# Reordering the seven products of a Strassen-type group, and the transfers around them, in a two-layer decoder trunk

## The chip, the cores and the metric

The kernel runs on one core of a Trainium2 chip. The metric is the device time of one execution in microseconds (us), the median of several runs. The core's engines work in parallel, each through its own queue in order: PE (TensorE, matrix products, with its weight loads shown as PEld), DVE (VectorE), ACT (ScalarE), POOL (GpSimd) and SP (SyncE, here only a queue that issues transfers). Transfers (DMA) are issued from SP and POOL and run on sixteen DMA engines.

## The reference, cut to what matters

Two layers of a decoder trunk on one sequence of 256 tokens with 1024 features, all in f32. Each layer is a half-weighted gated feed-forward (ffn1), a token mixer, a cross attention to a memory, and a second feed-forward (ffn2); each is preceded by an RMS norm and added to x:

```python
def swiglu(x, w_gate, w_up, w_down):
    return (jax.nn.silu(x @ w_gate) * (x @ w_up)) @ w_down

for l in range(DEPTH):                                   # DEPTH = 2
    x = x + 0.5 * swiglu(rmsnorm(x, ffn1_norm[l]), ffn1_w_gate[l], ffn1_w_up[l], ffn1_w_down[l])
    h = rmsnorm(x, mix_norm[l])
    x = x + (even_mixer(h, ...) if l % 2 == 0 else odd_mixer(h, ...))
    x = x + memory_cross_attention(rmsnorm(x, xa_norm[l]), mem_n, xa_w_q[l], xa_w_kv[l], xa_w_o[l])
    x = x + 0.5 * swiglu(rmsnorm(x, ffn2_norm[l]), ffn2_w_gate[l], ffn2_w_up[l], ffn2_w_down[l])
return rmsnorm(x, final_norm)
```

The hidden width of a feed-forward is 2816 = 22 x 128. The change lies in two of the four feed-forwards: ffn2 of layer 0 and ffn1 of layer 1, which follow one another.

## The kernel before, in words

**Weights.** All weights of the run are cut into 128x128 tiles and stored in HBM in the order of their use, in chunks of 16 tiles (1 MB). The class `Stream` loads chunk after chunk through SP's queue into four buffers `raw` and splits them block by block (8 tiles, 128x1024) into a high part `whi` (ACT, line 142) and the rest `wlo` (DVE, line 143). There are five buffers of each, so the splits run at most four blocks ahead of PE. A product of f32 values is made of three matmuls, high by high, low by high and high by low.

**A feed-forward stage** (`ffn`). Hidden features are made in groups of four tiles (f0 = 0, 4, 8, 12, 16) and a last group of two (f0 = 20). Of a group, the function `hidden` makes gate and up with the tokens on the partitions; each is cut into four parts of two row blocks (lines 560 to 562, 12 matmuls a part, cost 2600 ns with the planner). ACT applies the silu to the gate (line 581), DVE multiplies it with up. The result must then be turned, so that features lie on the partitions: `turned_back` transposes 32x32 blocks on DVE (line 531), writes the tile to HBM from POOL's queue (`turn`, line 533), reads it back with blocks exchanged in four transfers (line 535), and, some time later, splits it into the tiles h that the second product needs (ACT line 543, DVE line 544). The turned tile lies in one of two buffers, `v` or `kT`, in turns. This split is pinned in the order of ACT's and DVE's queues: what is behind it waits for it. The time at which it is put there is the delay given to `pe.after`. Then the down part multiplies h with the down weights (lines 417 and 418, the last column 422 to 424): four columns of x over the first 16 h tiles, the same four over h[16..19], over h[20..21], and then the other four whole.

**The seven products.** In the two stages named, group f0 = 12 is made with seven products instead of eight (Winograd's form): tokens are halved, input features are halved, and the two outputs (gate, up) stand as the other pair, so the weights are four quarters w11 (gate, upper rows), w21 (gate, lower rows), w12 (up, upper rows) and w22 (up, lower rows), a chunk of 1 MB each. Three products use a plain quarter, four use a sum of quarters. The sums are made by transfers of POOL's queue that add to what lies in the tile (line 617, `accum_op`): tile `one` (named k2) goes from w11 to w11+w12 to w11+w12+w22, tile `two` (named bias) from w12 to w12+w22, then w11 and w21 are added. These "added" chunks do not come through the stream. The inputs of four products are sums and differences of quarters of x (function `side`, lines 637 to 644), in buffers h. Each product is 12 matmuls into one bank `tr` (lines 665 to 667), and its result is kept in a tile h and combined on DVE and ACT (functions q1 to q7).

**What sets the order.** The class `Order` keeps a planned clock: fillers (the parts and products, in a written list) are emitted one after another, each advancing the clock by its cost, and tasks given to `after(delay, fn, cost)` are emitted before the first filler that starts at or after their due time. The list `ups` holds the parts of the groups 0, 4, 8, 16, 20; the seven products are inserted behind 10, 12, 14, 16, 18, 20 and 22 of the 36 parts. The framework's scheduler then may move instructions of one engine past each other, after a timing model of its own, unless an instruction is pinned with `tc.keep_in_program_order`: it then stays behind the instruction that was emitted before it on its engine.

Other users of the buffers: `bias` holds the values of the cross attention ahead of the first of the two stages, and behind the second the attention bias of the odd mixer (`load_bias`, line 1073, 1 MB read from `dists`); `k2` holds the keys of the cross attention.

Of the kernel before, what the change touches and what calls it, by code (L numbers as in the profile page):

```python
# [15 lines left out]
F32 = mybir.dt.float32  # L16
F32R = mybir.dt.float32r
AF = mybir.ActivationFunctionType
ALU = mybir.AluOpType
# [4 lines left out]
P = 128  # L24
D = 1024
KT = D // P
S = 256
FF = 2816
FT = FF // P
# [9 lines left out]
CHUNK = 16  # L39
# [225 lines left out]
def build(nc, tc, ctx, a):  # L265
# [18 lines left out]
    def w2():  # L284
        return act.tile([P, 512], F32, name="w2", bufs=6)
# [5 lines left out]
    x = consts.tile([P, KT, S], F32, name="x")  # L291
# [24 lines left out]
    def col(key, k):  # L316
        c = VCOL[key] + k
        return vecs[:, c:c + 1]
# [200 lines left out]
        nc.gpsimd.dma_start(out, tok.rearrange("(u q) f -> q u f", u=2))  # L519


    def ffn(which, layer, n, nxt, first=False, last=False):
        h = [None] * FT
        gate, up = f"{which}_w_gate", f"{which}_w_up"

        def turned_back(f0, s, c):

            t = act.tile([P, 8 * c * 32], F32, name=("v", "kT" if (which, layer) in AT else "k2")[f0 // 4 % 2], bufs=1)
            to = t.rearrange("p (b u c i) -> p u c b i", b=4, u=2, c=c)
            for u in range(2):  # L530
                nc.vector.transpose(to[:, u], s[u].rearrange("p (c b j) -> p c b j", c=c, b=4))
            d = dram.tile([P, 8 * c * 32], F32, name="turn", bufs=2)
            nc.gpsimd.dma_start(d, t)
            for b in range(4):
                nc.gpsimd.dma_start(t[32 * b:32 * b + 32].rearrange("j (a x) -> j a x", a=4),
                                   d.rearrange("(a j) (b x) -> b j a x", a=4, b=4)[b])
            back = t.rearrange("p (a u c i) -> p c u a i", a=4, u=2, c=c)

            def split():
                for i in range(c):  # L540
                    h[f0 + i] = x2 = h_tile()
                    hi, lo = (m.rearrange("p u (a i) -> p u a i", a=4) for m in (x2.hi, x2.lo))
                    tc.keep_in_program_order(nc.scalar.activation(hi, back[:, i], AF.Copy))
                    tc.keep_in_program_order(nc.vector.tensor_tensor(lo, back[:, i], hi.bitcast(F32), op=ALU.subtract))  # L544

            pe.after((18000 if (which, layer) in AT else 28000) if f0 < FT // 4 * 4 - 4 else 22000, split, 0)

        def rows_of(name, c, bank, evac, other=None):

# [49 lines left out]
                    rows_of(up, f0 * P, acc_tile, product))  # L599

        def seven(f0, at):

            at += 4
            w11, w21, w22 = (a["w"][ws.ring(at + 2 * i + 1)] for i in (2, 3, 5))
            w12 = a["w"][RING + list(AT).index((which, layer))]
            for p in range(4):
                for k in range(4):
                    ws.place.append((RING + list(AT).index((which, layer)), 4 * p + k,
                                     (up, layer, p * P, f0 * P + 2 * (k % 2 * P) + k // 2, 2)))
            one = act.tile([P, CHUNK * P], F32, name="k2", bufs=1)  # L610
            two = act.tile([P, CHUNK * P], F32, name="bias", bufs=1)
            nc.gpsimd.dma_start(one, w11)
            nc.gpsimd.dma_start(two, w12)
            done = []

            def add(t, w):
                tc.keep_in_program_order(nc.gpsimd.dma_start(t, w, accum_op=ALU.add))
# [12 lines left out]
            sides = {}  # L630

            def side(p):
                t, y = w2(), w1()[:, :P]
                s3, s1, s2, s4 = (t[:, i * P:(i + 1) * P] for i in range(4))
                g, gq = col(n.key, p), col(n.key, p + 4)
                (k0, k1), (q0, q1) = ((x[:, k, :P], x[:, k, P:]) for k in (p, p + 4))
                nc.vector.tensor_scalar(y, k1, g, None, op0=ALU.mult)
                nc.vector.scalar_tensor_tensor(s3, k0, g, y, op0=ALU.mult, op1=ALU.subtract)
                nc.vector.scalar_tensor_tensor(s1, q1, gq, y, op0=ALU.mult, op1=ALU.subtract)
                nc.vector.scalar_tensor_tensor(s2, q1, gq, s3, op0=ALU.mult, op1=ALU.add)  # L640
                nc.vector.scalar_tensor_tensor(s4, q0, gq, s2, op0=ALU.mult, op1=ALU.subtract)
                hi, lo = (act.tile([P, 512], F32R, name="h", bufs=FT) for _ in range(2))
                nc.scalar.activation(hi, t, AF.Copy)
                nc.vector.tensor_tensor(lo, t, hi.bitcast(F32), op=ALU.subtract)
                sides[p] = [[m[:, i * P:(i + 1) * P] for m in (hi, lo)] for i in range(4)]
# [12 lines left out]

            def product(left, evac, name=None, row=0):
                def go():  # L660
                    ps = tr_tile()
                    for p in range(4):
                        wh, wl = (paired(w) for w in ws.take(name, layer, row + p * P, f0 * P, 4))
                        xh, xl = left(p)
                        nc.tensor.matmul(ps, xh, wh, start=p == 0, stop=False)
                        nc.tensor.matmul(ps, xh, wl, start=False, stop=False)
                        nc.tensor.matmul(ps, xl, wh, start=False, stop=p == 3)
                    evac(ps)
                    ws.flush()

                return always, go, 2600

            def part(q, u):
                return lambda p: [n.x[p + 4 * q].v[:, u, m] for m in range(2)]

            def mixed(i):
                return lambda p: sides[p][i]
# [7 lines left out]
            def q7(ps):  # L685
                nc.scalar.activation(keep("q7"), ps, AF.Copy)
                add(two, w11)
                pe.after(10000, lambda: add(two, w21), 0)

            def q1(ps):  # L690
                nc.scalar.activation(keep("q1"), ps, AF.Copy)

            def q2(ps):
                s0 = keep("s0")
# [3 lines left out]
            def q6(ps):  # L698
# [6 lines left out]
            def q3(ps):  # L705
                t = kept["q1"]
                tt(t, ps, t, op=ALU.subtract)
                stt(t, t, r(0), kept["s0"], op0=ALU.mult, op1=ALU.mult)

            def q4(ps):  # L710
                t, u3 = kept["q5"], kept["q7"]
# [355 lines left out]
    def load_bias(which):  # L1067


        t = act.tile([P, 8, 256], F32, name="bias", bufs=1)  # L1070
        src = bass.AP(tensor=dists.tensor, offset=dists.offset + which * P * 8 * 384 + 127,
                      ap=[[8 * 384 - 1, P], [384, 8], [1, 256]])
        tc.keep_in_program_order(nc.gpsimd.dma_start(t, src))
        return t
# [341 lines left out]
```

## Time and profile before

| | |
|---|---|
| median of 3 runs | 980.32 us (979.98 to 980.7) |
| profiled execution | 980.3 us |
| its span, first to last instruction | 978.4 us, mean granted PE clock 0.993 |
| busy | PE 956.1 us (98%), PEld 872.4, DVE 715.3 (73%), ACT 573.3 (59%), POOL 130.0 (13%) |
| moved by DMA | 232.29 MB, 237 GB/s over the span |
| transfers issued from SP | 185.58 MB |
| transfers issued from POOL | 45.13 MB |

The profile's names leave out digits at the end: k2 is shown as k, w2 as w. A row of the timeline reads: start, duration, engine, line, operation, tile written <- tiles read, shapes, how often; in brackets the time that the engine was idle before it, and what ended that. A row of the waits reads: who waited on whom, us in all, times, longest. A row of stretches gives start and end, length, then busy us and instructions of PE, PEld, DVE, ACT and POOL, then the granted PE clock as a fraction, the share of the DMA engines in use, and GB/s. Lists of transfers give tile, queue, how many, size, and us from issue to landing.

### The profile page before, as it was taken

What the parts mean: (1) busy time and instruction counts of PE and PEld (TensorE: products, weight loads), DVE (VectorE), ACT (ScalarE), POOL (GpSimd) and SP (SyncE); (2) the same over time, 40 slices, a digit from 0 to 9 for tenths busy, and PEclk for the clock granted to TensorE, in tenths of its full rate; (3) what the DMA queues carried; (4) which work ended last, traced back from release to release, by engine and by line L of the source; (5) the groups of instructions that cost most, each with busy time, mean ns of one, the idle gap of its engine ahead of it and who ended that gap; (6) DMA issues with size and microseconds to landing.
All of it is one profiled execution on the core that took longest, in us unless ns stands there. A gap on an engine that the chain in (4) does not pass through costs nothing.

```text
span 978.4 us, 15160 instructions
## 1 busy us (share of the span) xinstructions
PE 956.1 (98%) x5808; PEld 872.4 (89%) x5808; DVE 715.3 (73%) x1152; ACT 573.3 (59%) x928; POOL 130.0 (13%) x229
## 2 busy tenths in 40 slices
PE   9999999999999899999999989999999999999997
PEld 8888899999999778879988867989999998888896
DVE  7667757888869769756967874766887797576673
ACT  7556545696657566544656545455786585555541
POOL 0411210001000121111011101100000005511210
PEclk9999999999999989999999999999999999999999
DMA  9899975545526899878679967955645357997831
GB/s 371 320 359 317 310 240 202 209 150 181 207 92 254 248 276 348 302 207 290 219 219 265 364 199 207 344 199 184 250 138 174 108 172 283 306 283 246 277 131 43
DMA packets 39191, 232.29 MB, mean 237 GB/s; under 512 B 5960, under 2 KB 6984, under 8 KB 14928
## 3 DMA queue, kind: packets, MB, share of 16 engines
q1 hardware_dynamic: 26784, 185.58, 52.8%
q0 software_dynamic: 11760, 45.13, 17.0%
q8 instruction: 45, 0.74, 0.3%
q10 hardware_dynamic: 576, 0.64, 0.2%
q14 instruction: 26, 0.21, 0.1%
HBM read 217.66 MB, written 16.80 MB: 240 GB/s over the span
## 4 chain that ended last, share of the span: by engine, by line
PE 75%; DMA 15%; issue 5%; DVE 2%; POOL 2%; ACT 1%; POOLq 0%; ACTq 0%; DVEq 0%
PE acc L561 8%; PE acc L560 7%; PE acc L562 7%; PE acc L422 7%; PE acc L424 7%; PE acc L423 7%; PE acc L417 6%; DMA turn<-kT 5%; DMA bias<-in_w 3%; DMA kT<-turn 3%; PE sc L417 3%; PE acc L418 3%; PE sc L560 2%; PE sc L561 2%; PE sc L562 2%
## 5 line engine op out<-in xcount | busy, mean ns | idle before, releaser
L143 DVE TENSOR_TENSOR wlo<-raw,whi 128x1024 fp32r<-128x1024 f32 (+2 forms) x373 | 419.2, 1136 | 149.4 <-ACT whi L142 146.8
L142 ACT ACTIVATE whi<-raw 128x1024 fp32r<-128x1024 f32 (+2 forms) x373 | 361.2, 982 | 236.4 <-PE acc L562 84.6
L561 PE MATMUL acc<-wlo,x 128*128 128x512 f32 x544 | 207.7, 382 | 3.0 <-DVE wlo L143 3.0
L560 PE MATMUL acc<-whi,x 128*128 128x512 f32 x544 | 203.5, 382 | 5.3 <-ACT whi L142 5.3
L562 PE MATMUL acc<-whi,x 128*128 128x512 f32 x544 | 206.5, 381 | 0.0
L560 PEld LDWEIGHTS acc<-whi,x 128*128 128x128 f32 x544 | 103.2, 190 | 21.4 <-ACT whi L142 7.1
L561 PEld LDWEIGHTS acc<-wlo,x 128*128 128x128 f32 x544 | 103.3, 190 | 19.8 <-DVE wlo L143 5.4
L562 PEld LDWEIGHTS acc<-whi,x 128*128 128x128 f32 x544 | 103.3, 190 | 14.5
L417 PE MATMUL acc<-h,whi 128*128 128x512 f32 x330 | 108.7, 382 | 2.4 <-DVE h L544 2.4
L418 PE MATMUL acc<-h,wlo 128*128 128x256 f32 x330 | 90.0, 273 | 0.0
L424 PE MATMUL acc<-h,wlo 128*128 128x256 f32 x322 | 87.7, 275 | 0.0
L423 PE MATMUL acc<-h,whi 128*128 128x256 f32 x322 | 87.7, 275 | 0.0
L422 PE MATMUL acc<-h,whi 128*128 128x256 f32 x322 | 86.5, 277 | 0.0
L424 PE MATMUL acc<-x,wlo 128*128 128x256 f32 x304 | 84.1, 278 | 0.0
L423 PE MATMUL acc<-x,whi 128*128 128x256 f32 x304 | 83.8, 277 | 0.0
L422 PE MATMUL acc<-x,whi 128*128 128x256 f32 x304 | 83.3, 278 | 0.0
L417 PEld LDWEIGHTS acc<-h,whi 128*128 128x128 f32 x330 | 62.4, 189 | 11.4 <-DVE h L544 2.7
L418 PEld LDWEIGHTS acc<-h,wlo 128*128 128x128 f32 x330 | 63.3, 192 | 0.1
L423 PEld LDWEIGHTS acc<-h,whi 128*128 128x128 f32 x322 | 61.7, 192 | 0.1
L424 PEld LDWEIGHTS acc<-h,wlo 128*128 128x128 f32 x322 | 61.7, 192 | 0.1
L422 PEld LDWEIGHTS acc<-h,whi 128*128 128x128 f32 x322 | 60.6, 192 | 0.4 <-DVE x L485 0.2
L423 PEld LDWEIGHTS acc<-x,whi 128*128 128x128 f32 x304 | 58.2, 192 | 0.2
(273 smaller groups left out, 1674.1 us busy)
## 6 DMA issues: line engine op xcount, KB each, us to landing
raw<-in_w SPq DMA_DIRECT2D x169, 1024.0 KB, 5.9
bias<-in_w POOLq DMA_DIRECT2D x8, 1024.0 KB, 14.5
turn<-v POOLq DMA_DIRECT2D x12, 512.0 KB, 3.4
v<-turn POOLq DMA_DIRECT2D x48, 128.0 KB, 6.1
k<-in_w POOLq DMA_DIRECT2D x6, 1024.0 KB, 10.4
dists<-line POOLq DMA_DIRECT2D x2, 1536.0 KB, 14.1
raw<-in_memT SPq DMA_DIRECT2D x3, 1024.0 KB, 4.9
raw<-in_w SPq DMA_DIRECT2D x7, 388.0 KB, 6.1
```

The costliest lines, as they stand in the source:

```text
L142: for ins in (self.nc.scalar.activation(hi[:, at], src, AF.Copy), self.nc.vector.tensor_tensor(lo[:, at], src, hi[:, at].bitcast(F32), op= ...
L143: self.nc.vector.tensor_tensor(lo[:, at], src, hi[:, at].bitcast(F32), op=ALU.subtract)):
L417: nc.tensor.matmul(ps, w[0], x2.both, start=start, stop=False)
L418: nc.tensor.matmul(ps[:, :S], w[1], x2.high, start=False, stop=stop)
L422: nc.tensor.matmul(ps[:, :S], w[0], x2.high, start=start, stop=False)
L423: nc.tensor.matmul(ps[:, :S], w[0], x2.low, start=False, stop=False)
L424: nc.tensor.matmul(ps[:, :S], w[1], x2.high, start=False, stop=stop)
L560: nc.tensor.matmul(ps[u], xh, wh, start=k == 0, stop=False)
L561: nc.tensor.matmul(ps[u], xh, wl, start=False, stop=False)
L562: nc.tensor.matmul(ps[u], xl, wh, start=False, stop=k == KT - 1)
```

## The change

- The products stand in another order, q1, q7, q2, q5, q3, q6, q4 instead of q5, q7, q1, q2, q6, q3, q4, and behind 4, 8, 10, 12, 16, 22 and 26 of the 36 parts.
- The first of them uses tile `one` while it still holds plain w11, so w11 is no longer loaded by the stream as well. w11 and w12 lie in two chunks of their own at the end (`RING`).
- The loads of `one` and `two` and the first sum (w12+w22) are in `load_bases`. For the first stage it is called at the stage's start, for the second 114 us (planned) into the first stage, there with all three pinned.
- The other sums are issued at the ends of q1, q7 (two of them, the second 18 us later) and q5.
- The mixed inputs are made in two halves, `side` at 8 us + 3.9 us a row block and `side2` at 32 us + 3.9 us; the first operation of each is pinned. q3 only copies its result, and q6 does the work that q3 did.
- The splits of turned tiles in these two stages stand 34 us behind the product for f0 = 0 and 4, 28 for f0 = 8 and 22 for 12, 16 and 20 (before: 18 for f0 below 16, 22 for the rest). The turned tile of f0 = 12 lies in k2 instead of kT.
- The read of the odd mixer's bias is planned 114 us into the second stage instead of 100 us.

```diff
+PLACES = (4, 8, 10, 12, 16, 22, 26)
-ADDED = {at + 4 + 2 * i + 1 for at in AT.values() for i in (0, 1, 4, 6)}
-RING = CHUNKS - len(AT)
+ADDED = {at + PLACES[i] // 2 + i for at in AT.values() for i in (0, 1, 3, 5, 6)}
+RING = CHUNKS - 2 * len(AT)
...
+    def load_bases(which, layer, pin):
+        w11, w12, w21, w22 = quarters(which, layer)
+        bases[which, layer] = tiles = [act.tile([P, CHUNK * P], F32, name=name, bufs=1) for name in ("k2", "bias")]
+        for t, w in zip(tiles, (w11, w12)):
+            ins = nc.gpsimd.dma_start(t, w)
+            if pin:
+                tc.keep_in_program_order(ins)
+        tc.keep_in_program_order(nc.gpsimd.dma_start(tiles[1], w22, accum_op=ALU.add))
...
-            t = act.tile([P, 8 * c * 32], F32, name=("v", "kT" if (which, layer) in AT else "k2")[f0 // 4 % 2], bufs=1)
+            t = act.tile([P, 8 * c * 32], F32, name=("v", "kT" if sevens and f0 != SEVEN else "k2")[f0 // 4 % 2], bufs=1)
...
-            pe.after((18000 if (which, layer) in AT else 28000) if f0 < FT // 4 * 4 - 4 else 22000, split, 0)
+            pe.after((34000 if f0 < 8 else 28000 if f0 < SEVEN else 22000) if sevens else
+                     28000 if f0 < FT // 4 * 4 - 4 else 22000, split, 0)
...
-            pe.after(6000, lambda: (add(one, w12), add(two, w22)), 0)
-            for i, t, n_added in ((0, one, 1), (1, two, 1), (4, one, 2), (6, two, 3)):
-                ws.sums[at + 2 * i + 1] = summed(t, n_added)
+            for i, t, n_added in ((0, one, 0), (1, two, 0), (3, one, 1), (5, one, 2), (6, two, 2)):
+                ws.sums[at[i]] = summed(t, n_added)
...
             def side(p):
                 t, y = w2(), w1()[:, :P]
-                s3, s1, s2, s4 = (t[:, i * P:(i + 1) * P] for i in range(4))
+                s3, s1 = (t[:, i * P:(i + 1) * P] for i in range(2))
...
+            def side2(p):
+                t = w2()
+                s2, s4 = (t[:, i * P:(i + 1) * P] for i in range(2))
...
             for p in range(4):
-                pe.after(8000 + 2600 * p, lambda p=p: side(p), 0)
+                pe.after(8000+3900*p, lambda p=p: side(p), 0)
+                pe.after(32000+3900*p, lambda p=p: side2(p), 0)
...
+            def q1(ps):
+                nc.scalar.activation(keep("q1"), ps, AF.Copy)
+                add(one, w12)
+
+            def q7(ps):
+                nc.scalar.activation(keep("q7"), ps, AF.Copy)
+                add(two, w11)
+                pe.after(18000, lambda: add(two, w21), 0)
...
-            return [product(mixed(1), q5), product(mixed(0), q7), product(part(0, 0), q1, gate),
-                    product(part(1, 0), q2, gate, 4 * P), product(mixed(2), q6), product(mixed(3), q3, up, 4 * P),
+            return [product(part(0, 0), q1), product(mixed(0), q7), product(part(1, 0), q2, gate, 4 * P),
+                    product(mixed(1), q5), product(mixed(3), q3, up, 4 * P), product(mixed(2), q6),
                     product(part(1, 1), q4)]
...
         if at is not None:
+            if (which, layer) == ("ffn2", 0):
+                load_bases(which, layer, False)
+                pe.after(114000, lambda: load_bases("ffn1", 1, True), 0)
             assert ws.taken == FIRST + at * CHUNK, (ws.taken, at)
             for i, f in enumerate(seven(SEVEN, at)):
-                ups.insert(8 + 2 + 3 * i, f)
+                ups.insert(PLACES[i] + i, f)
...
-    pe.after(100000, lambda: early.update(bias=load_bias(1)), 0)
+    pe.after(114000, lambda: early.update(bias=load_bias(1)), 0)
     ffn("ffn1", 1, n, nxt)
```

More of the change, by code (lines that the diff above doesn't have):

```diff
@@ L519, in to_tokens, with placed, quarters @@
         nc.gpsimd.dma_start(out, tok.rearrange("(u q) f -> q u f", u=2))
+    def placed(at):
+        return [at + o // 2 + i for i, o in enumerate(PLACES)]
+    def quarters(which, layer):
+        at, here = placed(AT[which, layer]), RING + 2 * list(AT).index((which, layer))
+        return [a["w"][c] for c in (here, here + 1, ws.ring(at[2]), ws.ring(at[4]))]
+    bases = {}
+    def load_bases(which, layer, pin):
[6 more added lines that the diff above has]
+        tc.keep_in_program_order(nc.gpsimd.dma_start(tiles[1], w22, accum_op=ALU.add))
     def ffn(which, layer, n, nxt, first=False, last=False):
@@ L524, in ffn @@
         gate, up = f"{which}_w_gate", f"{which}_w_up"
+        sevens = (which, layer) in AT
         def turned_back(f0, s, c):
-            t = act.tile([P, 8 * c * 32], F32, name=("v", "kT" if (which, layer) in AT else "k2")[f0 // 4 % 2], bufs=1)
+            t = act.tile([P, 8 * c * 32], F32, name=("v", "kT" if sevens and f0 != SEVEN else "k2")[f0 // 4 % 2], bufs=1)
             to = t.rearrange("p (b u c i) -> p u c b i", b=4, u=2, c=c)
@@ L601, in seven @@
         def seven(f0, at):
[L603 to L613, printed above, removed]
+            w11, w12, w21, w22 = quarters(which, layer)
+            at = placed(at)
+            for i, name in enumerate((gate, up)):
+                for p in range(4):
+                    for k in range(4):
+                        ws.place.append((RING + 2 * list(AT).index((which, layer)) + i, 4 * p + k,
+                                         (name, layer, p * P, f0 * P + 2 * (k % 2 * P) + k // 2, 2)))
+            one, two = bases[which, layer]
             done = []
@@ L624, in summed, with part_of @@
                 return ready
-            pe.after(6000, lambda: (add(one, w12), add(two, w22)), 0)
-            for i, t, n_added in ((0, one, 1), (1, two, 1), (4, one, 2), (6, two, 3)):
-                ws.sums[at + 2 * i + 1] = summed(t, n_added)
+            for i, t, n_added in ((0, one, 0), (1, two, 0), (3, one, 1), (5, one, 2), (6, two, 2)):
+                ws.sums[at[i]] = summed(t, n_added)
             sides = {}
+            def part_of(p):
+                return [(x[:, k, :P], x[:, k, P:], col(n.key, k)) for k in (p, p + 4)]
@@ L632, in side, with parted @@
+            def parted(t, at):
+                hl = act.tile([P, 512], F32R, name="h", bufs=FT)
+                hi, lo = hl[:, :S], hl[:, S:]
+                nc.scalar.activation(hi, t, AF.Copy)
+                nc.vector.tensor_tensor(lo, t, hi.bitcast(F32), op=ALU.subtract)
+                for i in range(2):
+                    sides[at[0], at[1] + i] = [m[:, i * P:(i + 1) * P] for m in (hi, lo)]
             def side(p):
                 t, y = w2(), w1()[:, :P]
-                s3, s1, s2, s4 = (t[:, i * P:(i + 1) * P] for i in range(4))
@@ L635, in side @@
-                g, gq = col(n.key, p), col(n.key, p + 4)
-                (k0, k1), (q0, q1) = ((x[:, k, :P], x[:, k, P:]) for k in (p, p + 4))
-                nc.vector.tensor_scalar(y, k1, g, None, op0=ALU.mult)
+                s3, s1 = (t[:, i * P:(i + 1) * P] for i in range(2))
+                (k0, k1, g), (q0, q1, gq) = part_of(p)
+                tc.keep_in_program_order(nc.vector.tensor_scalar(y, k1, g, None, op0=ALU.mult))
                 nc.vector.scalar_tensor_tensor(s3, k0, g, y, op0=ALU.mult, op1=ALU.subtract)
@@ L639, in side @@
                 nc.vector.scalar_tensor_tensor(s1, q1, gq, y, op0=ALU.mult, op1=ALU.subtract)
[L640 removed]
+                parted(t[:, :S], (p, 0))
+            def side2(p):
+                t = w2()
+                s2, s4 = (t[:, i * P:(i + 1) * P] for i in range(2))
+                (k0, k1, g), (q0, q1, gq) = part_of(p)
+                tc.keep_in_program_order(nc.vector.tensor_scalar(s2, k1, g, None, op0=ALU.mult))
+                nc.vector.scalar_tensor_tensor(s2, k0, g, s2, op0=ALU.mult, op1=ALU.subtract)
+                nc.vector.scalar_tensor_tensor(s2, q1, gq, s2, op0=ALU.mult, op1=ALU.add)
@@ L641, in side @@
                 nc.vector.scalar_tensor_tensor(s4, q0, gq, s2, op0=ALU.mult, op1=ALU.subtract)
[L642 to L645, printed above, removed]
+                parted(t[:, :S], (p, 2))
             for p in range(4):
-                pe.after(8000 + 2600 * p, lambda p=p: side(p), 0)
+                pe.after(8000+3900*p, lambda p=p: side(p), 0)
@@ L676, in mixed @@
             def mixed(i):
-                return lambda p: sides[p][i]
+                return lambda p: sides[p, i]
             tt, stt = nc.vector.tensor_tensor, nc.vector.scalar_tensor_tensor
+            def q1(ps):
[5 more added lines that the diff above has]
+                pe.after(18000, lambda: add(two, w21), 0)
             def q5(ps):
@@ L683, in q5, with q3 @@
                 add(one, w22)
[L685 to L691, printed above, removed]
+            def q3(ps):
+                nc.scalar.activation(keep("q3"), ps, AF.Copy)
             def q2(ps):
```

6 lines of the change are left out of this document (2 added, 4 removed).

## The prediction

> **What bounds the kernel now.** First I asked which engine the time belongs to: PE is busy 98% of the span (first row), and after the change it runs the same matmuls. So only places where PE waits, or runs at a lower clock, can give time. I read who PE waited for over the whole run, then cut the two changed stages (second feed-forward of layer 0, first of layer 1) at the first matmul of each part.
>
> ```profile
> PE 956.1 (98%) x5808; PEld 872.4 (89%) x5808; DVE 715.3 (73%) x1152; ACT 573.3 (59%) x928; POOL 130.0 (13%) x229
> ...
> PE acc L560 <- ACT whi L142: 5.3, 4, 3.3
> PE acc L561 <- DVE wlo L143: 3.0, 4, 0.8
> PE tr L665 <- ACT whi L142: 2.6, 2, 2.3
> PE acc L417 <- DVE h L544: 2.4, 1, 2.4
> PE tr L667 <- DVE h L644: 1.1, 1, 1.1
> ...
> 310.40:434.14 123.74, 117.04 (x520) 99.31 (x519) 90.24 (x125) 69.70 (x93) 18.26 (x28) 0.97 0.85 266
> 434.14:491.95 57.81, 57.81 (x376) 53.72 (x375) 46.38 (x73) 31.15 (x45) 5.47 (x10) 1.00 0.76 257
> 491.95:612.44 120.49, 114.35 (x521) 98.64 (x519) 84.84 (x113) 66.76 (x87) 16.48 (x27) 0.99 0.82 253
> 612.44:672.96 60.52, 58.08 (x376) 53.73 (x374) 42.58 (x62) 30.34 (x43) 6.26 (x11) 1.00 0.70 252
> 528.40:549.10 20.70, 20.70 (x97) 18.12 (x97) 17.67 (x21) 13.49 (x18) 1.42 (x2) 1.00 1.01 313
> ```
>
> The window rows give length, then busy time of PE, weight load, DVE, ACT and POOL, then PE's clock, DMA share and GB/s. Rows one and two are the up part and down part of the first stage, three and four those of the second. The last is undisturbed: 8 slots (a slot is 12 matmuls: half a quarter of an ordinary group, or one of the seven products) in 20.70 us, 2.59 us a slot. An up part has 36+7 = 43 slots, so 43 x 2.59 = 111.3 us, and 0.1 for two transposes. The losses are 123.74-111.4 = 12.3 and 120.49-111.4 = 9.1; the second down part is 60.52-57.81 = 2.7 us longer than the first, which has no PE wait. Together 24.1 us: the ceiling of what this change can give.
>
> Next I looked at what ACT, which works in order, stood in front of before each of PE's waits.
>
> ```profile
> 335.86 2.00 ACT L142 ACTIVATE whi<-k 128x1024 fp32r<-128x1024 f32 x2 [9.68 <-DMA k<-in_w]
> 343.32 2.00 ACT L142 ACTIVATE whi<-bias 128x1024 fp32r<-128x1024 f32 x2 [2.00 <-DMA bias<-in_w]
> 423.69 1.33 ACT L543 ACTIVATE h<-kT 128x256 fp32r<-128x256 f32 x4 [9.68 <-DMA kT<-turn]
> 568.43 1.33 ACT L543 ACTIVATE h<-kT 128x256 fp32r<-128x256 f32 x4 [8.73 <-DMA kT<-turn]
> 601.18 1.34 ACT L543 ACTIVATE h<-kT 128x256 fp32r<-128x256 f32 x4 [10.29 <-DMA kT<-turn]
> 640.86 0.72 ACT L543 ACTIVATE h<-kT 128x256 fp32r<-128x256 f32 x2 [6.32 <-DMA kT<-turn]
> ...
> 344.43 0.79 PE L665 MATMUL tr<-whi,h 128*128 128x512 f32 x1 [2.30 <-ACT whi L142]
> 345.02 0.63 PE L561 MATMUL sc<-wlo,x 128*128 128x512 f32 x1
> 345.44 0.63 PE L562 MATMUL sc<-whi,x 128*128 128x512 f32 x1
> 346.00:348.00 2.00, 2.00 (x6) 1.53 (x5) 1.50 (x2) 0.00 (x0) 2.00 (x5) 0.50 0.89 336
> ```
>
> Two kinds. The first two rows are a sum of weights that the split needs before it has landed (tiles k2 and bias). The others are a turned h tile whose split stands in ACT's queue before the tile is back; the weight splits behind it come late, and PE runs dry. After a wait PE also pays in clock: from 344.43 matmuls start 0.43 us apart, twice the usual 0.216 (20.70/96), at a granted clock of 0.50.
>
> **The change, part by part.** Times are in us from a stage's first up matmul, T; slots and delays are the code's, at 2.59 a slot.
>
> *Products and sums at the start.* Before, the first product starts at 10 slots (26 us) on w11+w12, and its sums queue on POOL behind the norm's rcol:
>
> ```profile
> 295.09 0.60 POOL L612 DMA_DIRECT2D k<-in_w  x1 [18.68 <-ACT w L896]
> 302.72 0.56 POOL L613 DMA_DIRECT2D bias<-in_w  x1 [7.03 <-PE tr L929]
> 322.33 1.61 POOL L385 TENSOR_TENSOR rcol<-ms,mhalf 128x2 f32<-128x2 f32 x1 [19.05 <-DVE ms L383]
> 323.90 0.91 POOL L617 DMA_DIRECT2D k<-in_w  x1
> 324.52 1.20 POOL L617 DMA_DIRECT2D bias<-in_w  x1
> ...
> k<-in_w POOLq DMA_DIRECT2D x1, 1024.0 KB, 5.2
> bias<-in_w POOLq DMA_DIRECT2D x1, 1024.0 KB, 7.9
> ...
> k<-in_w POOLq DMA_DIRECT2D x1, 1024.0 KB, 10.3
> bias<-in_w POOLq DMA_DIRECT2D x1, 1024.0 KB, 17.1
> ```
>
> (The landings 5.2 and 7.9 are of the loads at 295.09 and 302.72; 10.3 and 17.1 of a pair of sums issued together at 525.) Afterwards the first product, at 4 slots, needs plain w11: landed at 300.3, ten us before T. The second, at slot 9 (T+23.3 = 333.7), needs w12+w22. Its sum is pinned behind the w12 load, traced ahead of rcol, and that load landed at 310.6. So it goes out near 311 and lands by the longer row (17.1) at 328, by the shorter (10.3) at 321. ACT meets that split when block 6 is taken, T+13 = 323.5: it waits 0 to 5 us, with four blocks of split weights, ten us of PE work, in hand. Behind the sum's own wait on POOL stands only rcol, due 11 us later. The 9.68 and 2.00 waits go. If POOL takes rcol first, the sum leaves at 324 and lands at 334 to 341: PE waits 2 to 9 us. I take the early one, since its tile is ready 11 us before rcol.
>
> The other sums have room: w11+w12 goes out behind rcol near T+14 and lands by T+31 at 17.1 us; its split is due at T+31, PE at T+39. w22 goes onto it at T+42, landing by T+59, due T+60. On bias, w11 goes out at about T+33 and w21 at T+45, due T+73; behind w21's wait for w11 stands group 4's turn, not before T+56.
>
> *Second stage made ahead.* Before, its two loads were already issued early (374.32 below); only the sums waited, and PE lost nothing there. Afterwards two loads and one sum are pinned behind the first stage's last turned tile. Its return goes out at the latest 24 us into the down part (621.25+14.9 against 612.44 below), so they start by T+137 and, at 17.1 us each, end by T+188; the second stage begins at T+169. Its first product needs only the first load; its second needs the sum 13 us in, T+182: 6 us of ACT wait at that bound, none at the 12.0 that the sum of 323.90 took to 335.86 (T+173). That row is the nearer, since no three go out together, so nothing. Cover: the first down part has a DMA share of 0.76, 57.81 x 0.24 = 13.9 us free of all engines; 3 MB at 257 GB/s need 11.7.
>
> *Turned tiles and later splits.* Product ends before were at (group 0) 20.7, (4) 49.2, (12) 75.1, (8) 80.3, (16) 101, (20) 111.4, split 18 us later (22 for the last two). Groups 12 and 4 shared kT; 12 and 8 were turned nearly together. Afterwards 23.3, 51.8, (8) 77.7, (12) 85.4, 101, 111.4; splits after 34, 34, 28, 22, 22, 22; group 12 in k2.
>
> ```profile
> 374.32 0.55 POOL L612 DMA_DIRECT2D k<-in_w  x1 [0.55 <-DVE wlo L143]
> 404.48 0.56 POOL L533 DMA_DIRECT2D turn<-kT  x1 [14.52 <-DVE kT L531]
> 545.58 0.56 POOL L533 DMA_DIRECT2D turn<-kT  x1 [2.13 <-DVE kT L531]
> 580.58 0.57 POOL L533 DMA_DIRECT2D turn<-kT  x1 [17.58 <-DVE kT L531]
> 612.29 0.56 POOL L533 DMA_DIRECT2D turn<-v  x1 [17.68 <-DVE v L531]
> 620.33 0.93 POOL L1073 DMA_DIRECT2D bias<-dists  x1 [0.78 <-issue]
> 621.25 0.57 POOL L533 DMA_DIRECT2D turn<-kT  x1
> 626.97 1.34 ACT L543 ACTIVATE h<-v 128x256 fp32r<-128x256 f32 x4 [0.29 <-DMA v<-turn]
> ...
> bias<-dists POOLq DMA_DIRECT2D x1, 1024.0 KB, 13.6
> turn<-kT POOLq DMA_DIRECT2D x1, 256.0 KB, 14.9
> ```
>
> From turn issue to split ready: 568.43-545.58 = 22.9 (behind a sum), 423.69-404.48 = 19.2 and 601.18-580.58 = 20.6 (two tiles crossing), 626.97-612.29 = 14.7 undisturbed. Group 4 then has 34 us for 23+5: the 8.73 wait goes. Group 8 has 28 for at most 21+5. The 5 us from product to turn are an estimate: five dependent operations of 128x512, some 0.6 each by half of the 1.0 us of a 128x1024 split, and their queues. Group 12 has 24 to the slot boundary behind its due time (T+109): ready between 85.4+5+14.7 = 105 and 85.4+5+20.6 = 111. A down step takes 57.81/176 = 0.33 us, so PE needs group 12 at T+115, group 16 at T+132 and group 20 at T+138. ACT waits zero to 2 us; of PE's loss, 0 to 2, I take 1 us per stage, the middle.
>
> What is late next: group 8's split at T+106.5 now holds tile v past group 16's product (T+101), so that turn starts near T+109; before, it went out at 612.29 with the up part ending at 612.44, also T+111 without waits. Ready 14.7 to 20.6 later, T+124 to 130, ahead of T+132. Group 20 follows on POOL.
>
> *Bias behind the last tile.* 1 MB stood 0.92 us ahead of group 20's turn, which took 14.9 us; PE waited 2.4 for that h and the part ran 2.7 over. Behind the tile it holds nobody, and the odd mixer needs it only after the down part. I give 0.5 of the 2.7 back for the chain above.
>
> *The rest.* Mixed inputs are built in two halves: two more small DVE operations (0.34) and a second pair of splits per row block, under 1 us each of four; DVE has 123.74-90.24 = 33 us idle a stage. One more copy on ACT, which has 54 idle. One stream load a stage less. All hidden; if the cover fails at the crowded start, 0 to 3 us, I take 1, nearer the idle total.
>
> **Sum.** 980.3 (the profiled execution; median 980.32, so the same) - 24.1 + 2 (group 12) + 0.5 (group 20) + 1 (start) = 959.7.
>
> [...] After 2.30 us, behind two shorter waits, the clock fell to 0.50, so a leftover wait of 2 us may cost up to 5. [...]
>
> **Rivals.** (1) The first stage's sum still comes late (rcol first on POOL): 2 to 9 us more, 962 to 969; against it, the load's landing at 310.6, eleven us ahead of rcol. (2) The three MB in the first down part slow the weight stream, which shares the DMA engines: up to half of their 11.7 us comes back, 6 us, 966; against it, no PE wait on a stream load stands in the rows above. [...] (3) The stalls only move: the later splits lose what the old ones lost, 980; against it, 34 us for 28. (4) Slower: group 8's hold on v makes groups 16 and 20 late in both stages. With the worst rows (group 12 ready at T+111 and split before group 16's turn, which starts at T+115 and takes 22.9) h of group 16 is split at T+139, 7 us late; group 20's turn waits on POOL to T+132, takes 22.9 and is split at T+156, 11 us beyond its need. 18 us a stage, 36 in all, and 3 of half clock each: 980.3-24.1+36+6 = 998. It decides once the two waits pass 12 us a stage; for it speaks that v is held, against it that group 16 before stood at 626.97, undisturbed, 14.7 behind its turn.
>
> **How the numbers follow.** Forecast 0.70 (956 to 964); rival 1 0.13; rival 2 0.05; rival 3 0.04; rival 4 0.08. The range runs from no leftover (956.2) through rivals 1 and 2 to 970; about 0.12 is left out, and some for what I have not seen. A measurement of this kernel tells 0.2%, 2 us. Faster 0.88, same 0.04, slower 0.08.
>
> **What would show it.** Up parts of about 112 to 113 us and two down parts near 57.8; no wait of ACT on k or bias over 5 us; ACT's waits on turned tiles under 3 us; clock 1.00 throughout both stages; the read of dists behind the last return of kT. Wrong if PE waits on h at the head of a down part, or at the second product of the first stage.

## The result, and the profile after

The changed kernel took 956.77 us, median of 4 runs (956.45 to 956.96), and the kernel before 980.15 on the same chip (4 runs, 975.82 to 980.7): 0.9771 of its time, 95% interval 0.9743 to 0.9799. The forecast was 959.7, range 956 to 970. In the first group of experiments one execution of the kernel before ran at a granted clock of 0.946 and took 996.28 us; the ratios leave it out.

The profiled execution took 956.96 us with a span of 955.0, so 23.4 us of span are gone. The same views as before: the busy times, all waits of PE, and the four parts (up and down of the first stage, up and down of the second).

```profile
PE 947.9 (99%) x5808; PEld 869.8 (91%) x5808; DVE 720.6 (75%) x1176; ACT 577.2 (60%) x938; POOL 128.8 (13%) x229
```

```profile
PE tr L313 <- PEq L1407: 0.8, 1, 0.8
```

```profile
310.45:422.27 111.82, 111.82 (x520) 97.55 (x519) 94.22 (x138) 69.99 (x93) 17.69 (x27) 1.00 0.92 280
422.27:480.08 57.81, 57.81 (x376) 53.73 (x375) 42.22 (x64) 32.42 (x48) 6.88 (x12) 1.00 0.82 284
480.08:591.67 111.59, 111.59 (x521) 97.70 (x519) 90.49 (x133) 67.53 (x91) 15.90 (x26) 1.00 0.84 264
591.67:649.57 57.90, 57.90 (x376) 53.82 (x375) 41.82 (x63) 31.64 (x46) 5.83 (x10) 1.00 0.72 245
```

PE's only wait left is the 0.8 us at the start of the program. The four parts are shorter by 123.74-111.82 = 11.9, 0.0, 120.49-111.59 = 8.9 and 60.52-57.90 = 2.6: together 23.4, the whole of the difference. PE's busy time fell by 8.2 although the matmuls are the same number. About 4.8 of that is half clock, which the two stages no longer show: before, PE was busy for 9.6 us at 0.50 (from 343.79 to 350.62 and from 572.48 to 575.89). What makes the other 3.4 stays open. DVE and ACT have more work (5.3 and 3.9 us) and it shows nowhere.

What ACT meets now at the places of the old waits (its timeline; a bracket is idle time before the row):

```profile
326.06 2.01 ACT L143 ACTIVATE whi<-bias 128x1024 fp32r<-128x1024 f32 x2
415.67 1.32 ACT L564 ACTIVATE h<-v 128x256 fp32r<-128x256 f32 x4
422.04 1.34 ACT L564 ACTIVATE h<-k 128x256 fp32r<-128x256 f32 x4 [3.69 <-DMA k<-turn]
590.66 1.34 ACT L564 ACTIVATE h<-k 128x256 fp32r<-128x256 f32 x4 [2.91 <-DMA k<-turn]
615.13 0.72 ACT L564 ACTIVATE h<-kT 128x256 fp32r<-128x256 f32 x2 [1.35 <-DMA kT<-turn]
```

And POOL's queue around the first sum, the work made ahead, and the last tile:

```profile
310.93 0.90 POOL L539 DMA_DIRECT2D bias<-in_w  x1 [7.60 <-DMA bias<-in_w]
321.95 1.61 POOL L386 TENSOR_TENSOR rcol<-ms,mhalf 128x2 f32<-128x2 f32 x1 [10.12 <-DVE ms L384]
450.73 0.88 POOL L539 DMA_DIRECT2D bias<-in_w  x1 [13.03 <-DMA bias<-in_w]
606.88 1.63 POOL L556 DMA_DIRECT2D kT<-turn  x3 [8.48 <-DMA turn<-kT]
609.98 0.92 POOL L1111 DMA_DIRECT2D bias<-dists  x1
```

The first sum goes out at 310.93, eleven us ahead of rcol, lands 8.1 us later, and the split that needs it (326.06) finds it there. The second stage's first sum (450.73, behind its loads) goes out in the first down part, and no PE wait follows from it. The read of `dists` stands behind the last tile's return.

### The profile page after: what moved, and what is told of

Same layout as the page of the kernel before. It is cut to its first block, busy times and chain, and to the rows that moved or that the text cites. A ratio compares the mean times of both kernels' runs of the same rounds, so it can differ in the third digit from the quotient of the medians.

```text
span 955.0 us, 15188 instructions
## 1 busy us (share of the span) xinstructions
PE 947.9 (99%) x5808; PEld 869.8 (91%) x5808; DVE 720.6 (75%) x1176; ACT 577.2 (60%) x938; POOL 128.8 (13%) x229
## 4 chain that ended last, share of the span: by engine, by line
PE 99%; DVE 0%; POOLq 0%; DVEq 0%; issue 0%
PE acc L582 12%; PE acc L583 12%; PE acc L584 12%; PE acc L418 8%; PE acc L423 7%; PE acc L425 7%; PE acc L424 7%; PE acc L419 4%; PE sc L418 3%; PE sc L582 2%; PE sc L584 2%; PE sc L583 2%; PE acc L808 2%; PE sc L419 2%; PE acc L806 2%; PE acc L807 2%
## 5 line engine op out<-in xcount | busy, mean ns | idle before, releaser
L582 PEld LDWEIGHTS acc<-whi,x 128*128 128x128 f32 x544 | 103.0, 189 | 14.7 <-ACT whi L143 0.3
```

The source lines that it names most:

```text
L582: nc.tensor.matmul(ps[u], xh, wh, start=k == 0, stop=False)
```

## The experiments

Three theories were open. **A**: the stalls are separate, each part of the change removes its own, and the parts add up. **B** (rival 3 in small): taking away one stall only moves it, since what is late next takes its place. **C**: the order of the products itself matters, beyond the times at which its transfers and splits stand. Twelve runs follow in three groups, two of them repeats; within a group all are compared with the kernel before on the same chip.

### First group: parts of the change put into the kernel before

Here it took 978.73 us (23 runs, 975.94 to 984.52 but for the one at 996.28).

**Only the bias read moved.**

```diff
-    pe.after(100000, lambda: early.update(bias=load_bias(1)), 0)
+    pe.after(114000, lambda: early.update(bias=load_bias(1)), 0)
```

> The kernel before, with one thing of the change: the odd mixer's bias is read 114 instead of 100 us into the second stage. The theory (each PE wait comes from one late tile, and the parts add up) gives back the 2.7 us by which the second down part ran over, 977.6 us, with no PE wait at the end of that stage and the earlier waits as they were. The rival, that the last turned tile is late by itself, since its turn stands behind group 16's on POOL and the weight stream shares the DMA engines, gives 980 with ACT still waiting 4 us or more for it.

976.35 us (12 runs, 974.4 to 981.47), ratio 0.9977 [0.9958, 0.9997]: 2.4 us. POOL's timeline at the last tile of the second stage, and the one wait for an h that PE has left:

```profile
616.37 0.56 POOL L533 DMA_DIRECT2D turn<-kT  x1
...
629.41 0.92 POOL L1073 DMA_DIRECT2D bias<-dists  x1
```

```profile
PE acc L417 <- DVE h L544: 0.2, 1, 0.2
```

The wait of 2.4 for the last tile is gone, as the prediction had it: the 0.2 that is left stands at 461 us, in the down part of the first stage.

**Only the later splits and group 12's own buffer.**

```diff
-name=("v", "kT" if (which, layer) in AT else "k2")[f0 // 4 % 2]
+name=("v", "kT" if (which, layer) in AT and f0 != SEVEN else "k2")[f0 // 4 % 2]
...
-pe.after((18000 if (which, layer) in AT else 28000) if f0 < FT // 4 * 4 - 4 else 22000, split, 0)
+pe.after((34000 if f0 < 8 else 28000 if f0 < SEVEN else 22000) if (which, layer) in AT else
+         28000 if f0 < FT // 4 * 4 - 4 else 22000, split, 0)
```

> The kernel before, with only the later splits (34, 28 and 22 us) and the turned tile of group 12 in k2; products, sums and the read of the bias as before. From the stretches before, the waits on turned tiles cost 3.3 us behind the last product of the first stage and 9.1 in the second, 12.4 in all: the theory gives 967.9 us, and the wait at the first stage's start (9.0) and at the last tile (2.7) stay. The rival, that in the old order groups 12 and 8 cross (products 5 us apart) and group 12 is still too late, keeps 2 to 4 us per stage: 971 to 976.

965.63 us (963.66 to 965.96), 0.9855 [0.9836, 0.9874]: 13.1 us. Its two up parts:

```profile
310.09:431.14 121.05, 115.97 (x521) 99.53 (x519) 94.37 (x128) 71.19 (x93) 18.31 (x28) 0.97 0.89 285
488.94:600.53 111.59, 111.59 (x520) 97.70 (x519) 87.40 (x114) 67.95 (x87) 16.29 (x26) 1.00 0.90 283
```

The second stage is whole, its up part at 111.59; the first keeps the waits of the late sums and 9.5 us of loss. One thing came otherwise than expected: the 2.7 us at the last tile went too, although the bias read stands where it stood, since the tile's write now leaves ahead of that read (605.69 against 610.55) and PE has no wait in the second down part.

**Only the first stage's sums early.**

```diff
-            pe.after(6000, lambda: (add(one, w12), add(two, w22)), 0)
+            pe.after(6000 if layer else 0, lambda: (add(one, w12), add(two, w22)), 0)
```

> The kernel before, with the first two sums of the first stage issued straight behind their loads, ahead of the norm's rcol on POOL; everything else as before, the order of the products too. If the place of the sums on POOL's queue is what made them late, the 9.0 us at the start of the first stage go: 971.3 us. If the old order, which needs two sums at its first two products, is what made them late, PE still waits at the first product, 976 to 980.

977.4 us (10 runs, 975.69 to 979.34), 0.9978 [0.996, 0.9996]: 1.3 us and not the 9.0 expected. The start is repaired, and the gain is given back later in the same part (ACT's and PE's timelines, then the up part and four pieces of it of 3.4 us):

```profile
336.91 1.06 ACT L142 ACTIVATE whi<-bias 128x1024 fp32r<-128x1024 f32 x1 [1.16 <-issue]
391.35 1.03 ACT L543 ACTIVATE h<-kT 128x256 fp32r<-128x256 f32 x3 [9.40 <-DMA kT<-turn]
422.23 1.03 ACT L543 ACTIVATE h<-kT 128x256 fp32r<-128x256 f32 x3 [13.19 <-DMA kT<-turn]
393.68 0.48 PE L560 MATMUL acc<-whi,x 128*128 128x512 f32 x1 [2.47 <-ACT whi L142]
424.56 0.79 PE L560 MATMUL acc<-whi,x 128*128 128x512 f32 x1 [3.67 <-ACT whi L142]
```

```profile
310.54:433.17 122.63, 115.25 (x520) 99.28 (x519) 92.13 (x127) 70.97 (x93) 17.97 (x28) 0.97 0.86 274
389.51:392.93 3.42, 1.71 (x8) 1.14 (x7) 1.13 (x4) 1.58 (x5) 0.00 (x0) 1.00 1.01 400
392.93:396.34 3.41, 1.88 (x7) 1.43 (x8) 2.98 (x4) 2.59 (x3) 0.00 (x0) 1.00 0.22 89
420.23:423.65 3.42, 0.67 (x4) 0.23 (x2) 0.97 (x3) 1.42 (x5) 0.00 (x0) 1.00 0.77 173
423.65:427.06 3.41, 2.03 (x4) 1.35 (x5) 2.98 (x7) 2.96 (x6) 0.00 (x0) 0.50 0.01 4
```

ACT no longer waits for the sum (336.91). But the splits of the turned tiles then come earlier, and the tiles hardly do. ACT reaches group 4's split at 381.95 instead of 390.71, 8.8 us earlier, while its tile is back only 3.4 us earlier (391.35 against 394.72). So ACT waits 9.40 for group 4 (4.01 before) and 13.19 for group 12 (9.68 before), PE runs dry twice, and the second time the clock falls to 0.50. The up part is 122.63 instead of 123.74. B holds for this part alone: the early stall had hidden part of the later ones.

**All of them, in the old order of the products** (the three diffs together).

> The kernel before, with the later splits, group 12 in k2, the bias read at 114 us and the first stage's two sums ahead of rcol: all of the change but the order of the products, the plain first product, the halves of the mixed inputs and the second stage's sum made ahead. If the parts add up and the order is worth nothing by itself, 24.1 us go: 956 to 958 us, the time of the changed kernel. If the new order is needed to part the turns of groups 12 and 8, or to give the sums room, it stays 3 us or more behind the changed kernel: 960 or more.

956.63 us (956.22 to 956.98), 0.9767 [0.975, 0.9785]: 22.1 us. The three parts alone add up to 2.4+13.1+1.3 = 16.8, and in that the last tile counts twice, since the later splits alone repaired it too. Given the later splits, the early sums are worth 965.63-956.63 = 9.0 and not 1.3; given the early sums, the splits are worth about 20 and not 13 (both with the bias read moved as well, which the third group finds worth about 0.3 here). So the parts do not add up, as A had it; together they take away all the stalls, and B tells what each is worth alone. And C looks wrong already: the old order gives the time of the new.

### Second group: the changed kernel with one part undone

The kernel before took 978.61 us here (7 runs, 976.89 to 980.84). The changed kernel itself did not run on this chip; the losses below are against its 956.77, and the last kernel of this group, at 956.97 here, would make them 0.2 smaller.

**The old delays of the splits.**

```diff
-            pe.after((34000 if f0 < 8 else 28000 if f0 < SEVEN else 22000) if sevens else
+            pe.after((18000 if f0 < FT // 4 * 4 - 4 else 22000) if sevens else
```

> The changed kernel with the delays of before (18 us behind the product for groups 0, 4, 8 and 12, 22 for the last two); order, sums, k2 and bias as changed. By the changed kernel's trace group 4's tile is back some 27 us behind its product and group 12's 26, so ACT must stand 6 to 10 us at each; the theory (the delays carry it) gives PE waits of 2 to 4 us at group 4 with half clock behind them, 0 to 2 at group 12, per stage: 963 to 970. If the new order had made the tiles early enough, 957 to 959.

969.63 us (967.59 to 970.12), 0.9903 [0.9881, 0.9924]: against the 956.77 of the changed kernel 12.9 us of the gain are gone. A split on ACT, the PE wait behind it, and the first up part:

```profile
390.55 0.72 ACT L564 ACTIVATE h<-kT 128x256 fp32r<-128x256 f32 x2 [11.26 <-DMA kT<-turn]
392.88 0.48 PE L582 MATMUL acc<-whi,x 128*128 128x512 f32 x1 [4.32 <-ACT whi L143]
```

```profile
310.24:429.19 118.95, 113.85 (x521) 98.55 (x520) 92.84 (x137) 67.74 (x91) 17.69 (x27) 0.99 0.81 252
```

The same kind of wait as before the change, with the new order and the early sums in place: the delays are the larger part, not the order. Yet the order, or what came with it, is not worth nothing as long as the delays are the old ones: this kernel takes 969.63 where the early sums alone took 977.4 (first group, where the kernel before took 978.73). Of these 7.8 us the bias read explains some 2.4; the rest is the order, its other parts or the own buffer, and no run tells them apart.

**The first stage's sum behind rcol** (what rival 1 feared).

```diff
-        tc.keep_in_program_order(nc.gpsimd.dma_start(tiles[1], w22, accum_op=ALU.add))
+        pe.after(0 if pin else 6000, lambda: tc.keep_in_program_order(
+            nc.gpsimd.dma_start(tiles[1], w22, accum_op=ALU.add)), 0)
```

> The changed kernel with the first stage's sum w12+w22 issued behind the norm's rcol on POOL, as the sums were before (the second stage's stays ahead and pinned). The sum then leaves at 324 instead of 311 and lands at 333 to 341, and the second product waits for it: the theory gives 2 to 9 us, 959 to 966, with the whole of the wait on PE, since nothing else in the stage is late now. If the new order's plain first product had covered the late sum, 957.

959.24 us (958.68 to 959.91), 0.9803 [0.978, 0.9825]: 2.5 us more than the changed kernel. The split and PE's wait, and the first up part:

```profile
331.98 2.01 ACT L143 ACTIVATE whi<-bias 128x1024 fp32r<-128x1024 f32 x2 [6.14 <-DMA bias<-in_w]
336.08 0.70 PE L582 MATMUL sc<-whi,x 128*128 128x512 f32 x2 [1.04 <-ACT whi L143]
```

```profile
310.13:424.02 113.89, 112.56 (x521) 97.26 (x520) 94.05 (x138) 69.01 (x92) 17.73 (x27) 1.00 0.88 275
```

The sum leaves at 323.20, behind rcol as rival 1 had it, and is there at 332, 8.8 us later: a little sooner than even the short row (10.3) said. ACT waits 6.14, PE 1.04 and 0.3, and the part is 113.89-111.82 = 2.1 longer. Rival 1's mechanism is real and costs the lower end of its 2 to 9.

**The second stage's loads and first sum not pinned ahead**: that stage calls `load_bases` itself, unpinned.

```diff
-            if (which, layer) == ("ffn2", 0):
-                load_bases(which, layer, False)
-                pe.after(114000, lambda: load_bases("ffn1", 1, True), 0)
+            load_bases(which, layer, False)
```

> The changed kernel with the second stage's loads and first sum issued by the second stage itself, not pinned behind the first stage's last turned tile. The order of POOL's queue then has the load of bias and the sum, which waits for that load, between group 4's return and group 8's turn. The theory (what stands ahead of a turned tile on POOL and in its transfers makes it late) has group 8's turn go out about 5 us later and land behind the sum, group 12's behind it, and PE wait 2 to 8 us at the head of the first down part: 959 to 965. If the place does not matter, because the delays have room enough, 957.

961.3 us (959.6 to 961.61), 0.9818 [0.9798, 0.9838]: 4.5 us more than the changed kernel, but not for lateness of a sum. The scheduler moved the transfers forward, ahead of group 8's turn (POOL's and PE's timelines, then the first down part and two pieces of it):

```profile
396.59 0.90 POOL L539 DMA_DIRECT2D bias<-in_w  x1 [6.86 <-DMA bias<-in_w]
397.17 0.87 POOL L554 DMA_DIRECT2D turn<-v  x1
412.49 2.21 POOL L556 DMA_DIRECT2D v<-turn  x4 [14.46 <-DMA turn<-v]
414.70 0.57 POOL L554 DMA_DIRECT2D turn<-k  x1
428.82 0.56 PE L418 MATMUL acc<-h,whi 128*128 128x512 f32 x1 [2.41 <-DVE h L565]
```

```profile
422.32:484.55 62.23, 59.82 (x376) 55.03 (x375) 45.77 (x71) 34.27 (x52) 8.23 (x15) 0.97 0.73 244
425.68:429.09 3.41, 1.00 (x6) 0.68 (x5) 1.57 (x5) 1.20 (x4) 0.56 (x1) 1.00 0.65 213
429.09:432.50 3.41, 3.41 (x12) 2.87 (x12) 2.98 (x8) 3.41 (x6) 2.44 (x5) 0.50 0.35 76
```

POOL stands 6.86 us before the sum, and group 8's write to HBM behind that sum takes 15.0 us instead of the 3.9 that is the median of these tiles, landing 3.6 us after the sum (12.0 us from 396.59); group 12's write then cannot leave before 414.70. Its h comes 2.41 us too late at the head of the down part, and the part is 62.23-57.81 = 4.4 longer. What this part of the change buys is the place behind the last tile. The old order, which leaves the second stage's sums to that stage, gets along without it (third group).

**Group 12 in kT again.**

```diff
-name=("v", "kT" if sevens and f0 != SEVEN else "k2")[f0 // 4 % 2]
+name=("v", "kT" if sevens else "k2")[f0 // 4 % 2]
```

> The changed kernel with the turned tile of group 12 in kT again, which groups 4 and 20 use too. In the changed kernel's trace group 4's split is done 4 us before group 12's second transpose and group 12's 4 us before group 20's first, so the theory gives no difference, 956.5 to 957.5. If the buffer of its own is part of the gain, group 12 is 3 us or more later and PE waits at the head of the down part: 958 to 962.

956.97 us (956.72 to 957.65), 0.9778 [0.976, 0.9797]: no difference. In the new order the own buffer is not needed.

### Third group: is it the order?

The kernel before took 979.55 us here (11 runs, 976.7 to 982.29).

**The changed kernel once more.**

> The changed kernel again, beside the next one, to compare the two on one chip: 956 to 958 us by every theory.

956.69 us (956.43 to 956.98), 0.9764 [0.9744, 0.9784].

**The old order with the sums, the splits, the own buffer and the bias read** (the last kernel of the first group again).

> The kernel before with later splits, k2, bias last and early sums, in the old order of products, once more beside the changed kernel. If the new order is worth nothing, the two agree within 1 us (956 to 958); if it is worth something that the first pair of runs hid, they part by more than 1 us.

956.63 us (956.26 to 958.45), 0.9767 [0.9746, 0.9788]. On one chip the two lie 0.06 us apart, and in both PE's only wait left is the 0.8 at the start of the program. With the later splits and the early sums in place, the new order, the plain first product, the halves of the mixed inputs and the work made ahead are together worth nothing that can be measured. In that sense C is wrong.

**The same with the bias read at its old 100 us.**

> As the kernel with all but the order, but the bias read planned at 100 us as before. In the kernel with only the later splits the turn of the last tile already left ahead of that read, so the theory has the read harmless here, 956 to 958, with no PE wait at the last tile. If the read still stands in the way of the last tile's return (the read is now issued between the turn and the return), 958 to 960.

956.89 us (5 runs, 956.68 to 958.11), 0.9767 [0.9747, 0.9787]. Worth 2.4 us by itself, the bias read's place is worth about 0.3 here, which cannot be told from nothing. The timeline at the last tile (POOL, ACT):

```profile
596.85 0.56 POOL L533 DMA_DIRECT2D turn<-kT  x1 [3.15 <-DVE wlo L143]
...
602.98 0.93 POOL L1073 DMA_DIRECT2D bias<-dists  x1 [0.79 <-issue]
...
618.47 0.72 ACT L543 ACTIVATE h<-kT 128x256 fp32r<-128x256 f32 x2 [4.66 <-DMA kT<-turn]
```

The tile's write now leaves before the read instead of behind it; only its return meets the read. ACT waits 4.66 and PE 0.8, where PE lost 2.4 before. (The profiled execution is the longest of the five, 958.11.)

**And without the own buffer**, group 12 in kT.

```diff
-name=("v", "kT" if (which, layer) in AT and f0 != SEVEN else "k2")[f0 // 4 % 2]
+name=("v", "kT" if (which, layer) in AT else "k2")[f0 // 4 % 2]
```

> The kernel before with early sums and the new delays alone: group 12 in kT with groups 4 and 20, bias at 100 us. In the old order group 12's product ends 8 us before group 4's split at its new place, so kT holds group 12's turn back; its split at 97 us then finds the tile some 9 us away. The theory gives ACT waits of 6 to 12 us at group 12 and PE waits of 0 to 4 us per stage: 958 to 965. If only the delays count, 956 to 958.

961.01 us (6 runs, 957.41 to 964.84), 0.9812 [0.9787, 0.9837]. In the old order the buffer is worth some 4 us; the profiled execution is one of the long ones, 964.2. Its POOL and ACT rows, its wait and its first down part:

```profile
396.26 1.32 ACT L543 ACTIVATE h<-kT 128x256 fp32r<-128x256 f32 x4
401.70 0.56 POOL L533 DMA_DIRECT2D turn<-kT  x1 [17.21 <-DVE kT L531]
420.05 1.33 ACT L543 ACTIVATE h<-kT 128x256 fp32r<-128x256 f32 x4 [5.63 <-DMA kT<-turn]
429.30 0.56 POOL L533 DMA_DIRECT2D turn<-v  x1 [16.63 <-DVE v L531]
447.55 1.33 ACT L543 ACTIVATE h<-v 128x256 fp32r<-128x256 f32 x4 [9.78 <-DMA v<-turn]
```

```profile
PE acc L417 <- DVE h L544: 3.8, 1, 3.8
```

```profile
423.52:487.11 63.59, 59.76 (x376) 55.14 (x374) 46.58 (x77) 32.97 (x49) 5.48 (x10) 0.97 0.67 224
```

with, for comparison, the old order with the own buffer:

```profile
390.77 0.56 POOL L533 DMA_DIRECT2D turn<-k  x1 [7.83 <-DVE k L531]
408.00 1.32 ACT L543 ACTIVATE h<-k 128x256 fp32r<-128x256 f32 x4
423.81 0.55 POOL L533 DMA_DIRECT2D turn<-v  x1 [12.27 <-DVE v L531]
436.97 1.34 ACT L543 ACTIVATE h<-v 128x256 fp32r<-128x256 f32 x4 [0.35 <-DMA v<-turn]
```

Group 4 holds kT until its later split at 396.26, so group 12's tile is written 11 us later (401.70 against 390.77), its split comes 12 us later (420.05 against 408.00), and behind it in ACT's queue group 8's, which frees v; so group 16's tile is written 5.5 us later (429.30 against 423.81) and split 10.6 later (447.55 against 436.97), and PE waits 3.8 us. That is rival 4's chain (a later split holds a buffer past the next tile), started by kT instead of v. In the new order the numbers of the prediction say why it does not start: group 4's split is due at 51.8+34 = 85.8, just where group 12's last product ends (85.4), while in the old order it is 49.2+34 = 83.2 against 75.1.

So three edits carry the change: the first sum ahead of rcol, the later splits, and one way of keeping groups 4 and 12 apart, by the buffer or by the order. None of the versions is faster than the changed kernel by what can be told apart.

## Why the prediction was right

By its own steps:

- **The ceiling** (24.1 us, all in three parts). Right: the three parts gave 23.4 and the rest of the span nothing. The floor of 111.4 us for an up part, from 43 slots of 2.59, was met within 0.4 and 0.2.
- **The start** (1 us left). Mis-sized: 0.4 in the first up part, and no wait of PE. The sum went out at 310.93 (forecast near 311) and its split at 326.06 found it landed. The 1 us was chosen out of 0 to 3 without a row that measures it, and 0.4 came of it.
- **The second stage made ahead** (nothing). Right; the sum left at 450.73, T+140, and ACT did not wait for it.
- **Later splits** (waits gone, 1 us left for group 12 in each stage). The mechanism was right: group 8's splits at T+105 (forecast 106.5), group 16's at T+126 (124 to 130) without a wait. Group 12 was ready at T+111.6 and T+110.6, at and just past the late end of 105 to 111, and ACT waited 3.69 and 2.91 where "under 3" stood. The estimate of 5 us from product to turn was too small: the turns left at 404.13 and 573.53, 8.3 and 8.1 us behind the product's planned end at T+85.4; from there to the split they took 17.9 and 17.1, inside 14.7 to 20.6. But PE lost nothing: with its split weights in hand ahead, and h needed only at T+115, ACT's wait ended inside the cover. The term of 2 us was 1 a stage, the middle of a PE loss of 0 to 2 that was set equal to ACT's wait; what should have been priced is that wait less the cover, which is none.
- **Group 20 and the bias read** (0.5 left). The second down part took 57.90 against 57.81: 0.1. The 2.7 us went as forecast, though the experiments show two causes for it: the later splits let the write leave ahead of the read in any case, so moving the read adds almost nothing to them.
- **The sum.** Leftovers of 3.5 us were forecast and 0.7 remained. That is the 3 us between 959.7 and 956.8. That the time came out near the low end of the range although group 12 was later than estimated is the cover's doing, which the sum had left out: there it had luck.

What was wrong is not in the sum but beside it: the losses were read as belonging each to its own edit. Together the edits remove them all; singly they do not, as the third kernel of the first group showed, and its expectation of 9.0 us was the same error. The working also leaned on the new order (a plain first product, groups 8 and 12 turned apart); the old order with three edits reaches the same time, so these steps describe one way to it and not what it needs.

**The rivals.** Rival 1 did not come, and costs 2.5 us when made to. Rival 2 did not come: in the first down part POOL's queue moves 4.70 MB instead of 1.57, the stream's loads take 6.0 us to land instead of 4.9 (medians), and the part takes 57.81 us as before. That half of the 11.7 us would come back was an estimate, and no run shows it. Rival 3 holds for the early sums alone. Rival 4 did not come: group 16's split met no wait. Its chain was seen, with 3.8 us of PE wait where 18 a stage were forecast for the worst case, when kT was shared in the old order.

## What to carry to other kernels

An in-order engine that stands before a transfer cost PE here only what exceeded the work already split ahead: ACT's waits of 3.69 and 2.91 us in the changed kernel cost it nothing, and the 6.14 us of the late sum cost it 1.04 and 0.3. So give each such task a time at which its data is surely back. Stalls in series hide one another: a part worth 1.3 us alone was worth 9.0 (with the bias read's 0.3) once the next stall was gone, so parts of a change must be tried on top of each other as well as alone. A large transfer on a queue that also carries short, urgent ones should be pinned behind them; left free, the scheduler put it ahead here, a write took 15.0 us instead of 3.9, and the kernel 4.5 us more.

## What the runs showed of the hardware

- **The clock fell behind windows of 3.41 us in which PE was busy 1.02 us or less.** A single wait of 2.41 us, at the head of the down part of the kernel that was not pinned ahead, was followed by a clock of 0.50 and cost 4.4 us in all. Waits of 1.04 and 0.3 (the late sum) left the part at 1.00. The length of the wait alone does not decide: with only the sums early, the clock stayed at 1.00 through and behind a wait of 2.47. What sorts these cases is where the waits lie. In the kernel before, the clock fell to 0.50 at 343.79, 572.48 and 975.25 us, which are 67 and 118 times 3.413 us apart, and stayed there for 6.83 us, 3.41 us and up to the end of the program. With its span from 5.87 us on (99 such steps ahead of the first drop) cut into windows of 3.41 us along these times, PE was busy 0.92, 1.02 and 0.38 us of the window ahead of each drop, and at least 1.78 (from 565.66) of every other at a clock of 1.00. The rows of the two other kernels fit: PE was busy 1.00 us from 425.68 and 0.67 from 420.23, each with 0.50 behind it; the wait of 2.47 and the 0.78 behind it fall into two windows, busy 1.71 and 1.88, and no drop followed either. None of these windows lies between 1.02 and 1.71. So idle time of 2.4 us or more (3.41-1.02) in one such window costs, by an estimate from these rows, another 1.7 us (3.41 at half clock) or twice that (6.83). In the kernel before, the clock fell at 343.79, before the wait of 2.30 us ended at 344.43: the shorter wait of 1.13 ahead of it, which ended at 341.22, lies in the same window.
- **A write of 512 KB behind a 1 MB sum on POOL's queue** took 15.0 us from issue to landing in the kernel that was not pinned ahead, instead of the 3.9 that is the median of these tiles in the changed kernel; it landed 3.6 us after the sum.
- **In the third group the two kernels in which PE waits longest (15.2 and 5.0 us in their profiles, without the 0.8 at the start) spread the most from run to run.** The kernel before ranged over 5.6 us on one chip (976.7 to 982.29) and the shared buffer in the old order over 7.4, while the changed kernel stayed within 0.55 and the old order with all edits within 2.2 beside them. That the waits make the spread is not shown, and why landings vary from run to run stays open.
